# Hybrid decoder layer on eight cores: head-norm gains folded into the output gates, gated products left in PSUM, later side work, and a moved first weight load

## The chip, the cores and the metric

The kernel runs as one program on all eight NeuronCores of one Trainium2 chip. Each core takes one prompt of 2048 tokens and 16 samples of 4 tokens, so the cores do equal work on different data and do not talk to each other. The metric is the device time of the slowest core, in microseconds (us).

Some executions here were slower: the four cores of one die show a lower granted TensorE clock, 0.82 to 0.97 where the other die has 0.99 or 1.00. Each run below is marked fast or slow, and only fast runs are compared.

Names of engines in the profile: PE is TensorE's matrix multiplication and PEld its weight load, DVE is VectorE, ACT is ScalarE, POOL is GpSimd, SP is the engine that issues part of the transfers. PSUM (PS in the traces) is the memory that this program's matmuls write to, handed out by the program in eight banks; SBUF is the memory that holds its other tiles. An element of work in this kernel is usually a matmul with 512 columns, or an elementwise operation on a tile of 128 partitions by 512 float32 values (256 KB, 2 KB in each partition).

## The reference, cut to what matters

One layer, for a prompt group and a sample group with the same weights:

```python
h = x + 0.5 * swiglu(rmsnorm(x, norm_ffn1), w_ffn1_in, w_ffn1_out)
u = rmsnorm(h, norm_mix)
# u @ w_in gives q, k, v, r of two branches (gated linear attention, retention)
oa  = group_rmsnorm(oa, gn_gla, x.dtype) * jax.nn.silu(ra)      # gn_gla, gn_ret: the head norm weights
orr = group_rmsnorm(orr, gn_ret, x.dtype) * jax.nn.silu(gr)     # silu(ra), silu(gr): the output gates
mix = jax.nn.sigmoid(gate_a) * (oa @ w_out[:V_A]) + jax.nn.sigmoid(gate_r) * (orr @ w_out[V_A:])
h = h + mix
h = h + 0.5 * swiglu(rmsnorm(h, norm_ffn2), w_ffn2_in, w_ffn2_out)
h = h + (p @ w_ple_proj) * jax.nn.sigmoid(rmsnorm(h, norm_ple) @ w_ple_gate)    # input embedding
# after the layer: a final rmsnorm; the outputs are y and the new states
```

D_MODEL is 1024, the feed-forward width (FFN below) 2816, and there are four heads of value width 128 in each branch. A group norm of one block of 128 tokens therefore touches 4 heads x 128 value rows x 128 tokens.

## The kernel before

The program lists its operations with their estimated costs, and a list scheduler of its own then orders them on each engine, chooses buffers, and, for operations marked "flex", chooses between VectorE and GpSimd. So an edit in one place can move instructions elsewhere. The prompt is processed in two halves of two 512-token tiles; the sample group (64 tokens per core, "S" in tile names) is a third, small tile.

The start: activations are issued by the SP engine, the first two weight tiles, two pieces each, by GpSimd. A piece waits for the transfer named `first`, here the gains (GpSimd's first issue waits 3.0 us for it on core 6):

```python
first = dma("sp", gains[:], cpack[:], "c0", 34e3)
for q in range(4):
    xload(T[0].h, T[0], q, 4, ("x0", q))        # activations of the first tile, four pieces
xload(hS, T[4], 0, 1, "xS")                     # activations of the sample group
w0 = [piece(0, j, (first,)) for j in range(2)]  # first weight tile
w1 = [piece(1, j, (first,)) for j in range(2)]  # second weight tile
x1 = [xload(T[1].h, T[1], ..., (w1[0],)) for q in range(4)]   # second tile, after a weight piece
```

The end of an attention block: normalise, times the head norm weight, times the gate, one instruction for each head:

```python
tt(po, po, rs, ALU.mult, n)
for hl in range(4):
    gc = (G_GNA if br == 0 else G_GNR) + hl
    last = stt(t.q[br][:, hl, cs], po_.v(...), gains[:, gc:gc + 1], t.sr[br][:, hl, cs],
               ALU.mult, ALU.mult, bn)
```

The merge into the residual `h`. The gated product goes from PSUM into an SBUF buffer (`m1`, from a pool of 2 KB buffers called P2), and the add is "flex". The embedding stage has the same lines with `pp` for `pm`:

```python
S.limits = dict(..., gate=4, pm=3, ...)         # PSUM banks that a class of work may hold
(pg_, sg_), (pm_, m1_) = bundle("gate", PSUM, P2), bundle("pm", PSUM, P2)
... # pg: gate matmuls, sg: its tanh
... # pm: output projection matmuls
stt(m1, sg, 1.0, pm, ALU.add, ALU.mult, n)
tt(t.h[:, dm, :], t.h[:, dm, :], m1, ALU.add, n, eng="flex")
```

The second FFN of the first half is interleaved with `side`, a generator that emits what is left of the mixing, the states and the sample group's recurrence. One step of it is taken in every FFN step `k`. At the FFN's end the squares for the third tile's first normalisation are listed (`early[2] = full_norm(T[2])`), with nothing that keeps them from being scheduled earlier:

```python
for k, (g, t) in enumerate(seq):
    ...                                         # FFN matmuls of one group of columns
    if side is not None:
        next(side, None)
```

Of the kernel before, what the change touches and what calls it, by code (L numbers as in the profile page):

```python
# [30 lines left out]
TW = 2.5  # L31
BL = 150
# [632 lines left out]
def build_program():  # L665
# [100 lines left out]
    S.limits = dict(ffn=4, fo=3, fill=1, xp=2, qk=3, v=3, rg=2, gate=4, pm=3, po=2, sc=1, pu=1, ms=3, acc=3, accb=3, sq=3, mf=1, sqb=2, qt=1, up=1,  # L766
                    dec=6, rot=2, alow=1, st=4, tr=1, samp=3, sb=2, vb=1, pb=2)

    def bundle(cls, *pools):
        vts = [VT(p, cls) for p in pools]  # L770
        Bundle(vts, cls)
        return vts if len(vts) > 1 else vts[0]
# [13 lines left out]
    def act(out, in_, func, n, scale=1.0, bias=0.0):  # L786
        rd = [in_] + [x for x in (scale, bias) if not isinstance(x, float)]
        return S.op("act", lambda e: e.activation(out=res(out), in_=res(in_), func=func, bias=bias, scale=scale),  # L788
             rd, [out], dur=n * 0.000833 + (0.066 if inpsum(in_) else 0.095) + (0.0 if isinstance(scale, float) else 0.07), lat=0.2,
             tset=ACT_SET.get(func))  # L790
# [121 lines left out]
    first = dma("sp", gains[:], cpack[:], "c0", 34e3)  # L912
    for q in range(4):
        xload(T[0].h, T[0], q, 4, ("x0", q))
# [29 lines left out]
    class Norm:  # L944
        def __init__(self, t, direct=7, src=None):
            self.t, self.direct = t, direct
            self.src = t.h if src is None else src
            if direct:
                self.acc = bundle("acc", P2)

        def add(self, kc):
            t, n = self.t, self.t.n
            hk = self.src[:, kc, :]
            if kc < self.direct:

                a = self.acc.v(lambda x, n=n: x[:, 0:n])
                if kc == 0:
                    act(a, hk, AF.Square, n)
                    return
                q = bundle("sq", P2).v(lambda x, n=n: x[:, 0:n])  # L960
                act(q, hk, AF.Square, n)
                out = a
                if kc == self.direct - 1:
                    self.accb = bundle("accb", P1)
                    out = self.accb.v(lambda x, n=n: x[:, 0:n])
                tt(out, a, q, ALU.add, n, eng="flex")
                return
# [25 lines left out]
    def full_norm(t, direct=7, src=None):  # L993
        nm = Norm(t, direct, src)
        for kc in range(8 if direct < 7 else 7):
            nm.add(kc)
        return nm
# [3 lines left out]
    def ffn(tiles, next_gcol, lastk=LASTK, parts=None, then=None, side=None, plan=None, lead=None):  # L1001
# [5 lines left out]
        for k, (g, t) in enumerate(seq):  # L1007
# [14 lines left out]
            if side is not None:  # L1022
                next(side, None)
# [24 lines left out]
        if next_gcol == G_PLE and tiles[0].i == 0:  # L1048
            early[2] = full_norm(T[2])
# [15 lines left out]
    def mixing(hi, tiles, gtiles):  # L1065
# [111 lines left out]
        def rgate(t, r, br):  # L1177
            n = t.n
            for hl in range(4):
# [3 lines left out]
                act(t.sr[br][:, hl, :], p, AF.Silu, n)  # L1183

        def finish_o(t, br, b, po_, sqb_):
# [16 lines left out]
            for hl in range(4):  # L1202
                gc = (G_GNA if br == 0 else G_GNR) + hl
                last = stt(t.q[br][:, hl, cs], po_.v(lambda x, hl=hl, bn=bn: x[:, hl * bn:(hl + 1) * bn]),
                           gains[:, gc:gc + 1], t.sr[br][:, hl, cs], ALU.mult, ALU.mult, bn)
# [114 lines left out]
        def gate(t, br, dm, rg, ro):  # L1320
            n = t.n
            (pg_, sg_), (pm_, m1_) = bundle("gate", PSUM, P2), bundle("pm", PSUM, P2)
            pg, pm, sg, m1 = (x.v(lambda a, n=n: a[:, 0:n]) for x in (pg_, pm_, sg_, m1_))
# [7 lines left out]
            tt(t.h[:, dm, :], t.h[:, dm, :], m1, ALU.add, n, eng="flex")  # L1331
# [46 lines left out]
    def ple(hi):  # L1378
# [13 lines left out]
        def tile(t):  # L1392
# [6 lines left out]
            for dm in range(8):  # L1399
                (pg_, sg_), (pp_, m1_) = bundle("gate", PSUM, P2), bundle("pm", PSUM, P2)  # L1400
                pg, pp, sg, m1 = (x.v(lambda a, n=n: a[:, 0:n]) for x in (pg_, pp_, sg_, m1_))
# [11 lines left out]
                tt(t.h[:, dm, :], t.h[:, dm, :], m1, ALU.add, n, eng="flex")  # L1413
# [122 lines left out]
```

## Time and profile before

Three runs: 1512.15, 1514.57 and 1516.16 us, median 1514.57. The profiled run took 1515.37 us; its cores spanned 1506.6 to 1513.8 us.

| what | value | where read |
|---|---|---|
| TensorE busy | 97% of the span | page, part 1 |
| chain that ended last | 92% TensorE | page, part 4 |
| first FFN matmul starts | 24.8 to 27.7 us | timeline of each core |
| idle before the second FFN | 3.6 us, then a clock of 0.51 for 2.9 us | timeline, windows |
| VectorE, 512-column adds into `h` | 0.68 to 1.79 us | each such instruction, core 1 |

The page of the slowest core, number 6: its first line, the busy line of part 1 (engine, busy us, share, number of instructions), and the chain of work that ended last.

```profile
span 1513.8 us, 25283 instructions; the slowest of 8 cores (1506.6 to 1513.8 us)
PE 1465.8 (97%) x8720; PEld 709.7 (47%) x8875; DVE 682.4 (45%) x1330; ACT 565.6 (37%) x1053; POOL 197.4 (13%) x245
PE 92%; DVE 2%; issue 2%; ACT 2%; DMA 1%; SPq 0%; POOL 0%; DVEq 0%; ACTq 0%; POOLq 0%
```

TensorE bounds the kernel. No other engine matters by its busy time. Each can matter where TensorE waits for it, and a TensorE stall can cost twice, as the next lines show for this one: 3.61 us idle, and then matmuls at a lower clock. They are TensorE's timeline on core 6 (start, length of the merged group, operation, tiles; in brackets the idle time before it and what ended it).

```profile
487.79 3.19 PE L780 MATMUL PS<-u_47,ring_51 128*128 128x512 bf16 x14
494.58 0.57 PE L780 MATMUL PS<-T_2_100,ones 128*128 128x512 bf16 x1 [3.61 <-DVE T_2_100 L808]
...
495.37 4.73 PE L780 MATMUL PS<-u_47,ring_51 128*128 128x512 bf16 x15
```

Fourteen matmuls take 3.19 us before the stall of 3.61 us, and fifteen take 4.73 us after it: the granted clock is 1.00 from 485 us up to the stall, 0.51 from 494.6 to 497.5 us and 0.89 from there to 500 us. What it waited for stands in VectorE's timeline, same core:

```profile
489.51 1.12 DVE L808 TENSOR_TENSOR h_44<-h_44,T_0_104 128x512 f32<-128x512 f32 x1
...
491.34 1.43 DVE L808 TENSOR_TENSOR h_44<-h_44,T_7_111 128x512 f32<-128x512 f32 x1
492.69 1.75 DVE L808 TENSOR_TENSOR T_2_100<-T_11_115,T_0_104 128x512 bf16<-128x512 f32 x1
```

The same operation takes 0.69 us elsewhere. The window around it, with the columns' header (busy us and number of instructions of each engine, then the clock granted to TensorE and the share of DMA time):

```profile
core 6: us, PE busy (x) PEld busy (x) DVE busy (x) ACT busy (x) POOL busy (x), PEclk, DMA share, GB/s
475.00:500.00 25.00, 21.34 (x93) 9.02 (x93) 21.21 (x28) 17.29 (x27) 8.60 (x8) 0.93 0.44 73
```

A later wait on the same core, for work on the sample group (the prediction's third point):

```profile
547.88 0.30 PE L780 MATMUL PS<-T_8_112,kt_95 64*64 64x256 bf16 x2 [2.31 <-DVE T_8_112 L821]
```

```profile
27.50 1.89 PE L780 MATMUL PS<-u_47,ring_50 128*128 128x512 bf16 x8
```

### The profile page before, as it was taken

The numbers are of one execution on the slowest core, as the hardware profiler recorded it, in microseconds if no ns is written. First come the engines' busy times: TensorE is split into PE (matmuls) and PEld (weight loads), VectorE is DVE, ScalarE is ACT, GpSimd is POOL, SyncE is SP. The second block draws the span as 40 slices with busy tenths as digits, with TensorE's granted clock in tenths as the row PEclk, the third lists the DMA queues.
The fourth block names the chain that finished last, engine by engine and source line by source line (L and its number), as shares of the span: only waits on it lengthen the run. The fifth ranks groups of instructions, "written<-read, shape, count | busy, mean of one in ns | idle before, by whom it ended". The sixth has DMA issues, their size and how long they took to land.

```text
span 1513.8 us, 25283 instructions; the slowest of 8 cores (1506.6 to 1513.8 us)
## 1 busy us (share of the span) xinstructions
PE 1465.8 (97%) x8720; PEld 709.7 (47%) x8875; DVE 682.4 (45%) x1330; ACT 565.6 (37%) x1053; POOL 197.4 (13%) x245
## 2 busy tenths in 40 slices
PE   7999999999999999999999999999999999999996
PEld 2644444454444444444444444444444445444554
DVE  2322222649767633222683111253886752222367
ACT  3511111546765424311481111134675542121246
POOL 1000001002213100000230000000232310000032
PEclk8999999999999999999999999999999999999998
DMA  9833335441343486344677433544235326424104
GB/s 199 135 74 58 58 74 103 77 84 43 57 113 69 99 161 133 76 72 80 139 168 167 84 58 72 94 84 78 53 66 107 69 57 112 76 41 78 25 1 126
DMA packets 46860, 133.31 MB, mean 88 GB/s; under 512 B 5136, under 2 KB 27536, under 8 KB 37264
## 3 DMA queue, kind: packets, MB, share of 16 engines
q0 software_dynamic: 17616, 101.03, 38.1%
q1 hardware_dynamic: 29120, 30.65, 6.5%
q8 instruction: 74, 1.21, 0.3%
q14 instruction: 50, 0.41, 0.1%
HBM read 219.59 MB, written 13.11 MB: 154 GB/s over the span
## 4 chain that ended last, share of the span: by engine, by line
PE 92%; DVE 2%; issue 2%; ACT 2%; DMA 1%; SPq 0%; POOL 0%; DVEq 0%; ACTq 0%; POOLq 0%
PE PS L780 92%; DMA hS<-xP 1%; DVE u_47 L815 1%; ACT L788 1%; ACT PS L788 0%; PE PS L784 0%; SPq L838 0%; DVE T_2_100 L808 0%; DVE h_45 L815 0%; ACT T_0_104 L788 0%; DVE qR_90 L821 0%; DVE h_43 L815 0%; DVE T_0_104 L808 0%; DVE h_44 L808 0%; ACT T_9_113 L788 0%
## 5 line engine op out<-in xcount | busy, mean ns | idle before, releaser
L788 ACT ACT_TABLE_LOAD x90 | 115.5, 1283 | 27.5 <-PE PS L780 23.7
L780 PE MATMUL PS<-u_48,ring_54 128*128 128x512 bf16 x434 | 101.3, 384 | 0.7
L780 PE MATMUL PS<-u_47,ring_54 128*128 128x512 bf16 x436 | 100.3, 379 | 0.6
L780 PE MATMUL PS<-u_47,ring_52 128*128 128x512 bf16 x401 | 94.8, 379 | 0.8
L780 PE MATMUL PS<-u_48,ring_52 128*128 128x512 bf16 x406 | 94.1, 379 | 0.6
L780 PE MATMUL PS<-u_47,ring_50 128*128 128x512 bf16 x373 | 88.5, 379 | 0.7 <-issue 0.3
L780 PE MATMUL PS<-u_47,ring_51 128*128 128x512 bf16 x374 | 87.9, 383 | 0.6 <-issue 0.2
L780 PE MATMUL PS<-u_48,ring_50 128*128 128x512 bf16 (+1 forms) x407 | 86.4, 362 | 0.5
L780 PE MATMUL PS<-u_48,ring_51 128*128 128x512 bf16 (+1 forms) x410 | 85.6, 362 | 0.3
L780 PE MATMUL PS<-u_47,ring_53 128*128 128x512 bf16 x343 | 79.4, 379 | 0.5 <-issue 0.2
L780 PE MATMUL PS<-u_48,ring_53 128*128 128x512 bf16 x342 | 78.7, 379 | 0.7 <-ACT T_3_107 L788 0.2
L780 PEld LDWEIGHTS PS<-u_48,ring_54 128*128 128x128 bf16 x448 | 43.6, 99 | 52.5 <-issue 2.5
L780 PEld LDWEIGHTS PS<-u_47,ring_54 128*128 128x128 bf16 x448 | 42.7, 98 | 49.3 <-issue 1.1
L780 PEld LDWEIGHTS PS<-u_48,ring_52 128*128 128x128 bf16 x416 | 40.2, 98 | 47.8 <-issue 1.3
L780 PEld LDWEIGHTS PS<-u_48,ring_51 128*128 128x128 bf16 x416 | 40.5, 98 | 42.2 <-issue 0.4
L780 PEld LDWEIGHTS PS<-u_47,ring_52 128*128 128x128 bf16 x416 | 39.1, 98 | 44.8 <-issue 2.3
L780 PEld LDWEIGHTS PS<-u_48,ring_50 128*128 128x128 bf16 x416 | 40.3, 98 | 41.7 <-issue 0.2
L815 DVE SCALAR_TENSOR_TENSOR h_43<-PS,h_43 128x512 f32<-128x512 f32 (+2 forms) x37 | 22.7, 618 | 82.4 <-PE PS L780 77.4
L780 PEld LDWEIGHTS PS<-u_47,ring_51 128*128 128x128 bf16 x384 | 37.4, 99 | 45.1 <-issue 2.7
L780 PEld LDWEIGHTS PS<-u_47,ring_50 128*128 128x128 bf16 x384 | 36.9, 98 | 41.3 <-issue 0.4
L780 PEld LDWEIGHTS PS<-u_48,ring_53 128*128 128x128 bf16 x352 | 34.1, 98 | 40.6 <-issue 0.4
L780 PEld LDWEIGHTS PS<-u_47,ring_53 128*128 128x128 bf16 x352 | 33.5, 98 | 39.6 <-issue 1.9
(918 smaller groups left out, 2427.1 us busy)
## 6 DMA issues: line engine op xcount, KB each, us to landing
ring_52<-wflat POOLq DMA_DIRECT2D x14, 1024.0 KB, 9.8
ring_53<-wflat POOLq DMA_DIRECT2D x14, 1024.0 KB, 9.4
ring_54<-wflat POOLq DMA_DIRECT2D x14, 1024.0 KB, 9.3
ring_50<-wflat POOLq DMA_DIRECT2D x14, 1024.0 KB, 9.2
ring_51<-wflat POOLq DMA_DIRECT2D x12, 1024.0 KB, 9.1
ring_51<-wflat POOLq DMA_DIRECT2D x7, 704.0 KB, 6.0
ring_52<-wflat POOLq DMA_DIRECT2D x7, 704.0 KB, 6.1
ring_53<-wflat POOLq DMA_DIRECT2D x6, 704.0 KB, 6.4
```

The source lines that it names most:

```text
L780: return S.op("pe", lambda e: e.matmul(res(out), lhsT=res(lhsT), rhs=res(rhs), start=start, stop=stop, **kw), [lhsT, rhs], [out], dur=max( ...
L788: return S.op("act", lambda e: e.activation(out=res(out), in_=res(in_), func=func, bias=bias, scale=scale), rd, [out], dur=n * 0.000833 + ...
L815: return S.op("dve", lambda e: e.scalar_tensor_tensor(out=res(out), in0=res(in0), scalar=res(scalar), in1=res(in1), op0=op0, op1=op1), rd, ...
```

## The change

The intent, as its few words put it: head norm weights put into the output gates, gated products kept in PSUM, side work of the second FFN beginning later, the first weight load moved. In this document the four parts are called **gain**, **PSUM**, **side** and **first**. The diff, cut to its core (the embedding stage gets the same three edits as the merge; plumbing of the `after` argument is left out):

```diff
-    first = dma("sp", gains[:], cpack[:], "c0", 34e3)
-    for q in range(4):
-        xload(T[0].h, T[0], q, 4, ("x0", q))
+    dma("sp", gains[:], cpack[:], "c0", 34e3)
+    first = [xload(T[0].h, T[0], q, 4, ("x0", q)) for q in range(4)][0]
 ...
                 act(t.sr[br][:, hl, :], p, AF.Silu, n)
+                gc = (G_GNA if br == 0 else G_GNR) + hl
+                act(t.sr[br][:, hl, :], t.sr[br][:, hl, :], AF.Copy, n, scale=gains[:, gc:gc + 1])
 ...
-            for hl in range(4):
-                gc = (G_GNA if br == 0 else G_GNR) + hl
-                last = stt(t.q[br][:, hl, cs], po_.v(...), gains[:, gc:gc + 1], t.sr[br][:, hl, cs], ALU.mult, ALU.mult, bn)
+            last = tt(t.q[br][:, :, cs], po_.v(...), t.sr[br][:, :, cs], ALU.mult, n)
 ...
-    S.limits = dict(..., pm=3, ...)
+    S.limits = dict(..., pm=2, ...)
 ...
-            (pg_, sg_), (pm_, m1_) = bundle("gate", PSUM, P2), bundle("pm", PSUM, P2)
+            (pg_, sg_), pm_ = bundle("gate", PSUM, P2), bundle("pm", PSUM)
+            m1 = pm
 ...
-            tt(t.h[:, dm, :], t.h[:, dm, :], m1, ALU.add, n, eng="flex")
+            tt(t.h[:, dm, :], t.h[:, dm, :], m1, ALU.add, n)
 ...
+SKIP = 4
+EA = 1
-            if side is not None:
+            if k == SKIP:
+                mark["on"] = (S.ops[-1],)
+            if side is not None and k >= SKIP:
                 next(side, None)
 ...
-            early[2] = full_norm(T[2])
+            early[2] = full_norm(T[2], after=mark["on"] if EA else ())
```

More of the change, by code (lines that the diff above doesn't have):

```diff
@@ L765, in build_program @@
     S = Sched(bases)
-    S.limits = dict(ffn=4, fo=3, fill=1, xp=2, qk=3, v=3, rg=2, gate=4, pm=3, po=2, sc=1, pu=1, ms=3, acc=3, accb=3, sq=3, mf=1, sqb=2, qt=1, up=1,
+    S.limits = dict(ffn=4, fo=3, fill=1, xp=2, qk=3, v=3, rg=2, gate=4, pm=2, po=2, sc=1, pu=1, ms=3, acc=3, accb=3, sq=3, mf=1, sqb=2, qt=1, up=1,
                     dec=6, rot=2, alow=1, st=4, tr=1, samp=3, sb=2, vb=1, pb=2)
@@ L784, in transp, with act @@
         S.op("pe", lambda e: e.transpose(res(out), res(in_), res(idn)), [in_, idn], [out], dur=0.056, lat=0.265)
-    def act(out, in_, func, n, scale=1.0, bias=0.0):
+    def act(out, in_, func, n, scale=1.0, bias=0.0, after=()):
         rd = [in_] + [x for x in (scale, bias) if not isinstance(x, float)]
@@ L789, in act @@
              rd, [out], dur=n * 0.000833 + (0.066 if inpsum(in_) else 0.095) + (0.0 if isinstance(scale, float) else 0.07), lat=0.2,
-             tset=ACT_SET.get(func))
+             tset=ACT_SET.get(func), after=after)
     def acopy(out, in_, n, after=()):
@@ L944, in build_program, with __init__ @@
     class Norm:
-        def __init__(self, t, direct=7, src=None):
-            self.t, self.direct = t, direct
+        def __init__(self, t, direct=7, src=None, after=()):
+            self.t, self.direct, self.after = t, direct, after
             self.src = t.h if src is None else src
@@ L957, in add @@
                 if kc == 0:
-                    act(a, hk, AF.Square, n)
+                    act(a, hk, AF.Square, n, after=self.after)
                     return
                 q = bundle("sq", P2).v(lambda x, n=n: x[:, 0:n])
-                act(q, hk, AF.Square, n)
+                act(q, hk, AF.Square, n, after=self.after)
                 out = a
@@ L991, in to_u, with full_norm @@
             S.bias = 0
-    def full_norm(t, direct=7, src=None):
-        nm = Norm(t, direct, src)
+    def full_norm(t, direct=7, src=None, after=()):
+        nm = Norm(t, direct, src, after)
         for kc in range(8 if direct < 7 else 7):
@@ L1201, in finish_o @@
             cs = slice(b * 128, b * 128 + bn)
-            for hl in range(4):
-                gc = (G_GNA if br == 0 else G_GNR) + hl
-                last = stt(t.q[br][:, hl, cs], po_.v(lambda x, hl=hl, bn=bn: x[:, hl * bn:(hl + 1) * bn]),
-                           gains[:, gc:gc + 1], t.sr[br][:, hl, cs], ALU.mult, ALU.mult, bn)
+            last = tt(t.q[br][:, :, cs], po_.v(lambda x, n=n: x[:, 0:n].rearrange("p (h c) -> p h c", h=4)),
+                      t.sr[br][:, :, cs], ALU.mult, n)
             t.fin = (last,)
@@ L1321, in gate @@
             n = t.n
-            (pg_, sg_), (pm_, m1_) = bundle("gate", PSUM, P2), bundle("pm", PSUM, P2)
-            pg, pm, sg, m1 = (x.v(lambda a, n=n: a[:, 0:n]) for x in (pg_, pm_, sg_, m1_))
+            (pg_, sg_), pm_ = bundle("gate", PSUM, P2), bundle("pm", PSUM)
+            pg, pm, sg = (x.v(lambda a, n=n: a[:, 0:n]) for x in (pg_, pm_, sg_))
+            m1 = pm
             for kc in range(8):
@@ L1399, in tile @@
             for dm in range(8):
-                (pg_, sg_), (pp_, m1_) = bundle("gate", PSUM, P2), bundle("pm", PSUM, P2)
-                pg, pp, sg, m1 = (x.v(lambda a, n=n: a[:, 0:n]) for x in (pg_, pp_, sg_, m1_))
+                (pg_, sg_), pp_ = bundle("gate", PSUM, P2), bundle("pm", PSUM)
+                pg, pp, sg = (x.v(lambda a, n=n: a[:, 0:n]) for x in (pg_, pp_, sg_))
+                m1 = pp
                 wg = w[0 if dm < 4 else 2][:, :].rearrange("p (f k c) -> p f k c", k=8, c=128)
@@ L1412, in tile @@
                 stt(m1, sg, 1.0, pp, ALU.add, ALU.mult, n)
-                tt(t.h[:, dm, :], t.h[:, dm, :], m1, ALU.add, n, eng="flex")
+                tt(t.h[:, dm, :], t.h[:, dm, :], m1, ALU.add, n)
                 nm.add(dm)
```

## The prediction

> **What bounds the kernel now.** TensorE. The page shows PE 97% busy of 1513.8 us, VectorE 45%, ScalarE 37%; the chain of waits is 92% matmul. No large matmul is removed, so only PE's idle and slow-clock time can be won. On the profiled core (6), from the waits of PE, the timeline and the windows:
>
> - Start: the first FFN matmul begins at 27.7 us (24.8 on core 3, the fastest). It waited for the first normalisation, held up on ScalarE by the sample activations, which landed at 21 us, 16.4 us after issue, beside 4 MB (in the source) of weights. Those weights land 10 us before use.
> - Mixing to second FFN, 490.9 to 494.6 us: 3.6 us idle for one VectorE add (T_2_100). Sixteen matmuls then take about 0.43 us instead of 0.216: some 3 us at half clock. [...] the window's clock of 0.93 agrees. Before this stall residual adds ran on GpSimd (1.26 us), VectorE adds stretched from 0.69 to 1.1-1.8 us, and ScalarE squared the next tile (h_45).
> - 545.6 to 547.9: 2.3 us for sample states that landed 17 us after issue, with DMA 95% busy, and about 1.8 us of half clock. Most cores lack this.
> - Several waits of 0.5 to 1.8 us in attention, the embedding stage and the end, about 10 us.
>
> All mid-kernel losses together are about 25 us.
>
> **The change, costed.**
> - Head gain into the gate: 4 VectorE instructions of 0.28 us per block (1.12) become one of about 0.69; 32 blocks save some 14 us of VectorE. ScalarE gets 32 scalings of about 0.62 us (20 us). On the critical path: about 0 (+-2).
> - Gated product in PSUM, residual add always on VectorE: the add then has one SBUF input. [...] They should return to 0.69 us. But the two banks are held until the add is done, where three used to be: a risk of waits when an 8-instruction normalisation (5.4 us) sits in front.
> - Side work four steps later, h_45's squares deferred: empties the engines just where the 3.6 us stall is.
> - First weights wait for the first activation piece (about 7 us instead of 3.3): activations land about 3 us sooner; the weights have slack.
>
> **Sum.** Start -3; stall at 490 and its cold clock -5 (of 6.5); DMA stall -1; PSUM banks, ScalarE and tail +0.5. About -8.5 us, 0.6%.
>
> **Prediction:** 1506 us, 8 in 10 between 1498 and 1513. Faster by over 2% (below 1485): 0.01, since it exceeds all idle time reachable. Within 2%: 0.98. Slower by over 2%: 0.01.
>
> **Right if** the first FFN matmul starts near 24.5 us on all cores; PE is at 24 of 25 us or more and clock about 1.0 around the second FFN's start; additions into h take 0.69 us and none is on GpSimd; ScalarE busy rises about 20 us.
>
> **Wrong if** PE newly waits for PSUM additions in the gate or embedding stages (two banks); if the scaling delays attention on ScalarE; if PE waits for the first weights; or if the deferred squares only move the stall to where the third tile is normalised. The program orders its instructions by its own list scheduler, so unrelated places may shift by 1 or 2 us.

Two passages are cut, where marked. -3 -5 -1 +0.5 makes the -8.5 us. "The window's clock of 0.93 agrees" is the window of 25 us printed above, with 0.51 just after the stall. "They should return to 0.69 us" (the adds of 1.1 to 1.8 us) stands as the estimate. The trace of before supports it: on core 6 the 512-column VectorE operations of this kind (TENSOR_TENSOR) with one input in PSUM took 0.69 us in the mean, 19 of them beside GpSimd work (at most 0.70) and 247 with GpSimd idle.

## More of the kernel before

A norm adds up its squares with further "flex" additions of two SBUF operands. GpSimd therefore has elementwise work even where it adds nothing into `h`.

The start of core 1: the waits of TensorE up to 30 us, the longest two lines; the first FFN matmul in the timeline; and the two DMA queues from 12 to 17 us, where q0 carries the weights and q1 the activations (packets, MB, share of the time of the 16 DMA engines).

```profile
PE PS L780 <- ACT T_0_98 L788: 4.6, 2, 3.0
PE PS L780 <- DVE Sbf L835: 2.7, 1, 2.7
```

```profile
q0 software_dynamic: 163, 0.60, 71.0%
q1 hardware_dynamic: 163, 0.52, 29.9%
```

T_0_98 holds the square of a piece of activations: the wait is really one for the transfer of that piece.

## The result, and the profile after

Four runs: 1493.50, 1493.67, 1493.92 and 1493.95 us, median 1493.8, against 1515.37 us, the median of four runs of before (the three above and one more of 1517.17). All are fast, with a granted clock of 0.995 to 0.997 on every core. The ratio is 0.986, with a 95% interval of 0.9842 to 0.9877. Here and below a ratio is the mean time of one kernel's fast runs over that of the other's of the same rounds, so not quite the ratio of the medians that are quoted. Executions in which one die ran at a lower clock are left out of the means. The change won 21.6 us by the medians, 1.4%. "Within 2%" was right, but the time lies 4 us below the low end of the predicted range.

The page of the slowest core after, number 1:

```profile
span 1491.9 us, 25299 instructions; the slowest of 8 cores (1489.9 to 1491.9 us)
PE 1468.5 (98%) x8875; PEld 708.5 (47%) x8875; DVE 666.2 (45%) x1281; ACT 578.2 (39%) x1084; POOL 136.2 (9%) x192
PE 93%; DVE 2%; ACT 1%; issue 1%; DMA 1%; POOL 0%; DVEq 0%; SPq 0%; ACTq 0%; POOLq 0%
```

TensorE's timeline before the second FFN, and its window:

```profile
481.12 3.19 PE L782 MATMUL PS<-u_47,ring_51 128*128 128x512 bf16 x14
484.60 0.38 PE L782 MATMUL PS<-T_5_103,ones 128*128 128x512 bf16 x1 [0.29 <-DVE T_5_103 L810]
```

```profile
475.00:500.00 25.00, 24.71 (x116) 11.08 (x114) 17.13 (x28) 10.52 (x16) 2.38 (x3) 1.00 0.49 86
```

The 3.61 us are 0.29 us now, and the clock is whole. The start of core 1: the longest two waits, the first FFN matmul, and the queues from 7 to 12 us.

```profile
PE PS L782 <- DVE Sbf L837: 2.7, 1, 2.7
PE PS L782 <- ACT T_0_98 L790: 1.5, 1, 1.5
```

```profile
19.22 1.89 PE L782 MATMUL PS<-u_47,ring_50 128*128 128x512 bf16 x8
```

```profile
q1 hardware_dynamic: 459, 1.51, 94.1%
q0 software_dynamic: 4, 0.02, 1.8%
```

The first FFN matmul starts 8.3 us sooner on this core (over the cores: 16.6 to 19.2 us, where it was 24.8 to 27.7). The activations had nearly the whole of the DMA to themselves: 94.1% of the time of the 16 engines, and 1.51 MB in these 5 us.

The elementwise work, by group of instructions (busy us, mean ns of one, idle before): first a finishing product of before on core 6, then the new one, the new scalings on ScalarE and an addition into `h`, on core 1 of after.

```profile
L815 DVE SCALAR_TENSOR_TENSOR qR_79<-PS,gains,sr 128x128 bf16<-128x128 f32 x32 | 9.0, 344 | 0.5
```

```profile
L810 DVE TENSOR_TENSOR qR_79<-PS,sr 128x512 bf16<-128x512 f32 x8 | 5.5, 689 | 0.6
L790 ACT ACTIVATE sr<-sr,gains 128x512 f32<-128x512 f32 x16 | 11.3, 722 | 1.1
L810 DVE TENSOR_TENSOR h_43<-h_43,PS 128x512 f32<-128x512 f32 x40 | 26.8, 683 | 1.8
```

### Where the time came from

For each core whose trace has a record of every matmul, I took the start of each matmul and subtracted the ideal time of the program's matmuls before it: 216 ns for 512 columns, as they follow each other in the trace at full clock, in proportion for fewer columns, but not below 29 ns (the 64-column matmuls follow each other after 29 ns in the trace of core 1); the filler matmuls of the start are left out. What remains is TensorE time lost up to that point, idle or at a lower clock. The columns cut the program at fixed amounts of matmul work, so at the same stages in every kernel: the start up to 25 us of matmul work; the first FFN and the first half's mixing up to 450; the second FFN of the first half up to 625; its end and the embedding up to 750; the second half's first FFN and attention up to 1125; the rest. Only differences between rows are read. (A figure can be negative, since the ideal time is only an estimate for small matmuls.) The mean is over the six of the eight cores with complete records; before and after these are the same six, all but cores 0 and 6 (the experiments' six are partly others).

```
us of TensorE lost    start  to 450  450-625  625-750  750-1125   rest   mean span
before                 27.8     8.4      2.0      1.7       7.4   15.8      1509.0
after                  19.8     7.9     -3.1      0.8       5.9   14.1      1491.2
difference             -8.0    -0.5     -5.1     -0.9      -1.5   -1.7       -17.8
```

The differences add up to the 17.7 us that the mean core won (17.8 unrounded). The slowest core of the profiled run won 21.9 (1513.8 to 1491.9), since it lay 4.8 us above this mean before and 0.7 us after.

### The profile page after: what moved, and what is told of

The parts are those of the page before. It is cut to its first block, busy times and chain, and to the rows that moved or that the text cites. A ratio compares the mean times of both kernels' runs of the same rounds, so it can differ in the third digit from the quotient of the medians.

```text
span 1491.9 us, 25299 instructions; the slowest of 8 cores (1489.9 to 1491.9 us)
## 1 busy us (share of the span) xinstructions
PE 1468.5 (98%) x8875; PEld 708.5 (47%) x8875; DVE 666.2 (45%) x1281; ACT 578.2 (39%) x1084; POOL 136.2 (9%) x192
## 4 chain that ended last, share of the span: by engine, by line
PE 93%; DVE 2%; ACT 1%; issue 1%; DMA 1%; POOL 0%; DVEq 0%; SPq 0%; ACTq 0%; POOLq 0%
PE PS L782 93%; DVE u_47 L817 1%; ACT L790 1%; DMA h_43<-xP 0%; ACT PS L790 0%; DMA rtab_116<-rtab 0%; PE PS L786 0%; POOL T_2_100 L810 0%; DVE T_5_109 L810 0%; DVE h_43 L817 0%; DVE qR_90 L823 0%; DVE T_0_104 L810 0%; DVE T_10_114 L810 0%; DVE PS L817 0%; DVE T_2_106 L810 0%
## 5 line engine op out<-in xcount | busy, mean ns | idle before, releaser
L790 ACT ACT_TABLE_LOAD x81 | 103.9, 1283 | 23.3 <-PE PS L782 20.5
L782 PE MATMUL PS<-u_47,ring_54 128*128 128x512 bf16 x448 | 103.1, 379 | 0.0
L782 PE MATMUL PS<-u_48,ring_54 128*128 128x512 bf16 x448 | 100.8, 379 | 0.0
L782 PE MATMUL PS<-u_47,ring_52 128*128 128x512 bf16 x416 | 97.0, 379 | 0.0
L782 PE MATMUL PS<-u_48,ring_52 128*128 128x512 bf16 x416 | 94.6, 379 | 0.1
L782 PE MATMUL PS<-u_47,ring_50 128*128 128x512 bf16 x384 | 89.8, 379 | 0.0
L782 PE MATMUL PS<-u_47,ring_51 128*128 128x512 bf16 x384 | 87.8, 379 | 0.0
L782 PE MATMUL PS<-u_47,ring_53 128*128 128x512 bf16 x352 | 81.7, 379 | 0.1
L782 PE MATMUL PS<-u_48,ring_53 128*128 128x512 bf16 x352 | 79.4, 379 | 0.0
L782 PEld LDWEIGHTS PS<-u_48,ring_54 128*128 128x128 bf16 x448 | 43.6, 98 | 51.4 <-issue 0.4
L782 PEld LDWEIGHTS PS<-u_47,ring_54 128*128 128x128 bf16 x448 | 42.3, 98 | 47.4 <-issue 0.7
L782 PEld LDWEIGHTS PS<-u_48,ring_52 128*128 128x128 bf16 x416 | 40.5, 98 | 48.4 <-issue 1.2
L782 PEld LDWEIGHTS PS<-u_48,ring_51 128*128 128x128 bf16 x416 | 40.5, 98 | 42.2 <-issue 0.4
L782 PEld LDWEIGHTS PS<-u_47,ring_52 128*128 128x128 bf16 x416 | 39.2, 98 | 44.5 <-issue 2.0
L782 PEld LDWEIGHTS PS<-u_48,ring_50 128*128 128x128 bf16 x416 | 40.0, 98 | 41.9 <-issue 0.7
L782 PEld LDWEIGHTS PS<-u_47,ring_51 128*128 128x128 bf16 x384 | 37.1, 98 | 43.8 <-issue 0.8
L782 PEld LDWEIGHTS PS<-u_47,ring_50 128*128 128x128 bf16 x384 | 36.6, 98 | 41.2 <-issue 1.4
L782 PEld LDWEIGHTS PS<-u_48,ring_53 128*128 128x128 bf16 x352 | 34.1, 98 | 40.5 <-issue 0.4
L790 ACT ACTIVATE PS<-PS 128x512 f32<-128x512 f32 (+4 forms) x90 | 44.9, 509 | 20.1 <-PE PS L782 16.7
```

What stands on the lines that cost most here:

```text
L782: return S.op("pe", lambda e: e.matmul(res(out), lhsT=res(lhsT), rhs=res(rhs), start=start, stop=stop, **kw), [lhsT, rhs], [out], dur=max( ...
L790: return S.op("act", lambda e: e.activation(out=res(out), in_=res(in_), func=func, bias=bias, scale=scale), rd, [out], dur=n * 0.000833 + ...
```

## The experiments

Two kinds: one part of the change put into the kernel before (labels with d), and one part taken out of the changed kernel (labels with u). Every result was correct. Every kernel was timed against runs of the kernel before on the same chip; medians below are of the fast runs (15 of the 77 executions of the experiments were slow and are left out). The chips differ a little: the median of before was 1513.0 to 1513.9 us on four occasions and 1517.2 us on one chip, of which more below. Letters in the quoted expectations name theories; where it helps they are explained after the quotes.

The table of losses for the experiments on undisturbed chips, in the same columns (two cores each of d_first and d_pm2 had one stretch of 4 us at a clock of 0.81, which costs under 1 us):

```
us of TensorE lost    start  to 450  450-625  625-750  750-1125   rest   mean span
d_first                19.9     8.7      3.1      1.8       7.6   15.8      1502.7
d_gain                 27.3     8.4      1.7      1.9       5.2   16.2      1506.5
d_psum                 27.4     8.2     -3.0      1.2       7.5   14.3      1501.5
d_side                 27.4     8.2     -2.5      1.8       7.4   16.3      1504.5
d_pm2                  27.7     8.0      1.1      2.0       6.2   18.2      1509.1
u_first                27.4     7.9     -3.1      0.8       5.9   14.1      1498.8
u_gain                 20.0     8.2     -3.1      0.8       7.1   14.4      1493.2
u_psum                 19.6     8.0     -2.2      1.8       5.5   15.5      1493.9
u_side                 19.4     7.9     -3.2      1.4       5.9   14.2      1491.3
u_hold                 19.2     7.9     -3.1      0.8       5.9   13.9      1490.5
u_tosb_pm2             19.8     7.7     -3.0      2.6       5.2   18.4      1496.4
u_pm3                  19.7     7.5     -3.2      4.6       6.2   16.9      1497.6
u_tosb2                19.6     7.9     -2.4      6.0       5.7   18.1      1500.9
u_vec                  20.1     9.4     -2.0      6.3      12.4   22.1      1514.0
```

### The moved first weight load: d_first, u_first

d_first is the kernel before with the first hunk of the diff alone; u_first is the changed kernel with that hunk undone.

```diff
-    first = dma("sp", gains[:], cpack[:], "c0", 34e3)
+    first = [xload(T[0].h, T[0], q, 4, ("x0", q)) for q in range(4)][0]
```

> The kernel before with one edit: the first weight pieces wait for the first activation piece instead of the gains. The order of instructions on every engine is unchanged by it (compared before this run), so only the wait differs. Theory (the weight reads took the larger share of the DMA engines from the activations of the first normalisation, which were needed first; the weights had slack): the sample activations land near 13 us instead of 21, the weights at the same times as before (about 16, 19, 23, 26 us), the first FFN matmul starts near 18 to 19 us, and the whole is 8 to 9 us faster, about 1507 us; every stage after the start loses what it lost before. Rival (the two queues share evenly, as the prediction assumed; the rest of the early gain comes from the other edits' reordering): 3 us faster, about 1512, first matmul near 24.5.

> The changed kernel with only this edit undone (again the same order on every engine). Theory: 8 to 9 us slower than the changed kernel, about 1502, and the cores spread again by some 3 us, because their start depends on when the activations land. Rival: about 1497.

Measured: d_first 1506.06 us (1505.79 to 1512.21, three fast runs), ratio 0.9964 with an interval of 0.9932 to 0.9995; u_first 1502.3 us (four fast runs), ratio 0.9919 (0.9904 to 0.9934). The order of the instructions of d_first is that of before on every engine, so only the wait differs. The start column shows it alone: 27.8 to 19.9 us when it is added, 19.8 to 27.4 us when it is taken away. So this part is worth some 8 us at the start, alone and in company; of the mean span it wins 6.3 us alone and costs 7.6 us when taken away. Most of the rest of the 8 us in d_first is lost again in the second FFN (3.1 us against 2.0), where the expectation had no change: the single cores of the profiled run have 1.5 to 5.2 us there, and core 7 waits 2.0 us for work on the sample group, as core 6 does before. One of the three fast runs came out 6 us longer than the others, by one core (core 3, 1510.7 us). That run has no trace, so its cause is not shown.

### Why so much at the start: d_half, u_late

In d_half, the kernel before lets the second weight tile alone wait for the first activation piece; the first weight tile goes as early as before. In u_late, the changed kernel lets all weights wait for the fourth activation piece instead of the first.

```diff
 d_half, from before:
-    w1 = [piece(1, j, (first,)) for j in range(2)]
+    w1 = [piece(1, j, (xfirst,)) for j in range(2)]     # xfirst: the first activation piece
 u_late, from after:
-    first = [xload(T[0].h, T[0], q, 4, ("x0", q)) for q in range(4)][0]
+    first = [xload(T[0].h, T[0], q, 4, ("x0", q)) for q in range(4)][3]
```

> The kernel before, with only the second weight (two pieces) made to wait for the first activation piece; the first weight still starts at once. Same order on every engine. Theory Q (weight pieces are served one after the other, and whichever is being served takes most of the DMA engines; the first weight alone is busy until about 19 us): the activations land as late as before, sample activations at 19 to 21 us, first FFN matmul 25 to 28 us, total 1513 to 1516. Rival V (the activations are slowed in proportion to all the weight bytes in flight): half the gain, sample activations near 17 us, first matmul near 23, total about 1510.

> The changed kernel with the weights held for the last (fourth) activation piece, about 12 us, instead of the first, about 7 us. The scheduler moves some filler matmuls at the start with it. Theory: the activations hardly land sooner (12 to 13 us, as in the changed kernel), the weights land 3 to 4 us later, their slack is used up, and the second tile's activations, which wait for the second weight, land later too; first FFN matmul near 20 to 21 us, total 1495 to 1498. Rival (the weights' time still doesn't matter): 1493 to 1495.

These ran, with d_noflex and u_tosb, on a chip where TensorE's clock fell to 0.81 in stretches even in fast runs: a 512-column matmul then follows the last after 263 ns and not 216. On core 2 of u_late the granted clock is 0.81 from 740 to 750 us, 1.00 from 755 to 765 us and 0.81 again from 775 to 780 us, with TensorE busy for 39.9 of the 40 us. That cost up to 8 us on single cores, so times are compared within this chip only, where before took 1517.2 us. The start column is early enough to be free of it.

Measured: d_half 1519.6 us, ratio 1.0012 (0.9989 to 1.0035), start 27.5 us: no gain. u_late 1507.0 us, ratio 0.9929 (0.9907 to 0.9952), start 27.9 us: the whole 8 us are gone, which the expectation had not seen (it had the first matmul right, at 20 to 21 us, and a loss of 2 to 4 us in all). Times from issue to landing on core 1 explain all four (each entry is the moment of issue > the moment of landing, in us, worked out from the trace's transfer records):

```
            4th piece, tile 0   samples       weight pieces (2 of tile 0, 2 of tile 1)              tile 1, last
before      2.9>17.0            3.5>20.8      3.8>15.4   4.5>19.0   5.0>22.7   5.5>25.9             25.2>34.3
d_half      2.9>17.6            4.7>21.3      3.7>15.4   4.4>18.8   8.1>22.5   8.7>25.7             25.0>34.2
after       2.9>12.4            4.5>13.1      7.9>16.3   8.6>19.5   9.2>22.9   9.7>25.7             25.4>33.5
u_late      2.9>12.2            4.2>12.8     12.8>20.1  13.5>24.0  14.0>27.1  14.5>30.8             28.7>38.2
```

Three things are seen here. Before, the first weight piece overlaps the activations; from 12 to 17 us the two queues moved 163 packets each (core 1; 177 and 164 on core 0, 159 and 156 on core 6), but the weight packets took 71% of the time, so the activations crawled: 0.52 MB in these 5 us, where after moves 1.51 MB from 7 to 12 us. With 5 us of 16 engines, a weight packet took 0.35 us (71% of 80 us, over 163) and an activation packet 0.15 us; for the packets of 4096 bytes alone it is 0.39 and 0.18 us. Second, the weight pieces land one after another, 3.2 to 3.7 us apart in before. d_half issues the second tile's pieces 3.1 us later, and the activations land no sooner (17.6 and 21.3 us, against 17.0 and 20.8), so it is the first tile's pieces that matter. Third, in after the weights land within 0.9 us of where they landed before, although issued 4.1 us later; the first packet of the first piece came 5.3 us after its issue in before, 4.0 us in after and 2.6 us in u_late (core 1; why these waits differ, no run here shows). The later start used up their slack: in u_late the first piece lands 3.8 us later still, and the second tile's activations, which wait behind a weight piece, 4.7 us later. TensorE's timeline of u_late on core 1, and its window:

```profile
22.52 11.82 PE L782 MATMUL PS<-u,ring 128*128 128x512 bf16 x54
...
45.37 10.84 PE L782 MATMUL PS<-u,ring 128*128 128x256 bf16 x76 [3.54 <-DVE u L817]
```

```profile
45.00:50.00 5.00, 4.63 (x22) 2.54 (x23) 4.70 (x14) 4.65 (x8) 0.00 (x0) 0.50 1.04 174
```

The first FFN matmul waits until 22.5 us (19.2 in after; over the cores 18.5 to 22.5, mean 20.0, where after has 18.2), and at 45.4 us the normalised second tile is 3.5 us late, and TensorE is at half clock from 43.4 to 50.2 us (0.50 in the window). So only some 2 of the 8 us are the first tile's; most are the second tile's wait and the half clock with it. The change's choice, the first piece, is right between the two that were tried.

### Gains in the gates: d_gain, u_gain

The second and third hunks of the diff, alone in before, and undone in after:

```diff
+                act(t.sr[br][:, hl, :], t.sr[br][:, hl, :], AF.Copy, n, scale=gains[:, gc:gc + 1])
-            for hl in range(4):
-                last = stt(..., gains[:, gc:gc + 1], t.sr[br][:, hl, cs], ALU.mult, ALU.mult, bn)
+            last = tt(t.q[br][:, :, cs], po_.v(...), t.sr[br][:, :, cs], ALU.mult, n)
```

> The kernel before with the head norm weights folded into the gates alone (32 large ScalarE scalings more, one VectorE product in place of four per block). Theory A (neither engine bounds the attention stages for long): 1513 to 1517, within 2 us of before, changes only between the two attention stages. Rival B (the shorter VectorE chain in attention frees TensorE): 3 us faster or more, with the waits of TensorE in the attention stage of the second half gone. Rival C (ScalarE, 24 of 25 us busy there, becomes the limit): 2 us slower or more.

> The changed kernel with the fold undone. Theory A: within 2 us of the changed kernel, 1492 to 1496. Rival B: 1497 or more. Rival C: 1492 or less.

Measured: u_gain 1496.8 us (three fast runs), ratio 0.9882 (0.9865 to 0.9898). d_gain had only one fast run, 1509.68 us; its other three were slow (up to 1742 us, one die at a clock of 0.84), so it has no ratio and is read from its profile, which is of the fast run. Both say the same: about 2 us in the mean span (1509.0 to 1506.5; 1493.2 against 1491.2), most of it in the second half's attention (7.4 to 5.2; 7.1 against 5.9), where the prediction had 0. So theory A, no change, is missed by both; d_gain's one run lies 4 us under the median of before on its chip, as rival B had it, and u_gain at 1496.8 just under B's line of 1497. Rival C, ScalarE as the new limit, falls. The windows over that stage on core 1, before and then d_gain:

```profile
1010.00:1185.00 175.00, 170.98 (x1079) 81.09 (x1078) 122.12 (x262) 101.03 (x187) 34.43 (x40) 1.00 0.42 76
```

```profile
1010.00:1185.00 175.00, 173.37 (x1119) 83.54 (x1118) 115.49 (x223) 114.60 (x210) 37.41 (x43) 1.00 0.42 75
```

VectorE has 6.6 us less to do, ScalarE 13.6 us more, and TensorE is busy 2.4 us more. The window ends after different work in the two, so the table is the better measure of the size; the direction is the same. In the first half's attention little or nothing was won (8.4 and 8.4 us; 8.2 against 7.9).

### The product in PSUM, and the side work: d_psum, u_psum, d_side, u_side

d_psum has the three edits of the PSUM part in both stages and nothing else; d_side has the SKIP and EA lines and nothing else. u_psum and u_side undo them.

```diff
 d_psum: pm=3 becomes pm=2; m1 = pm (and m1 = pp); eng="flex" taken from the two adds into h
 u_side: SKIP = 0 and EA = 0 in the changed kernel
```

> The kernel before with the gated products kept in PSUM and the residual add fixed on VectorE alone (two product banks instead of three). Theory P (the 3.6 us stall before the second FFN and the half-clock matmuls after it come from residual adds on GpSimd and from VectorE adds stretched by GpSimd): that stall is under 1 us, the embedding stage loses about 1 us less, total about 1508 to 1510. Rival S (they come from the third tile's squares and the sample work that crowd ScalarE and VectorE just then): the stall stays, total 1513 or more. Rival B (two banks are too few): new waits of TensorE on VectorE in the gates, total above 1516.

> The changed kernel with this part undone. Theory P: the stall of 3 us or more is back before the second FFN, about 1499. Rival S: stays below 1496.

> The kernel before with the later side work and the deferred squares alone. Theory P: the stall before the second FFN stays at 2 us or more, since the adds on GpSimd remain; total 1512 to 1515. Rival S: the stall goes, total about 1509 to 1510.

> The changed kernel with the side work begun at once and the squares not deferred. Theory P: below 1496. Rival S: 1498 or more, the stall of 3 us or more is back. If both d_psum and d_side remove the stall, either suffices; if neither does, both are needed.

| kernel | median us | ratio to before, 95% interval |
|---|---|---|
| d_psum | 1505.2 | 0.9945 (0.9930 to 0.9961) |
| u_psum | 1497.4 | 0.9893 (0.9875 to 0.9911) |
| d_side | 1509.1 | 0.9970 (0.9949 to 0.9992) |
| u_side | 1494.5 | 0.9874 (0.9859 to 0.9890) |

Either part alone removes the loss in the second FFN stage: 2.0 us becomes -3.0 with PSUM and -2.5 with side, and in company -3.1. Taking either away leaves it removed (-2.2 and -3.2). So theory P (the adds alone make the stall) is refuted by d_side and u_psum, rival S (the side work alone makes it) by d_psum and u_side, and rival B (two banks are too few) by d_psum. The windows on core 1 (before has 21.39 us busy and a clock of 0.93 there, and a stall of 3.61 us), of d_psum and then d_side, and the one wait of TensorE that d_side has left in its window:

```profile
475.00:500.00 25.00, 24.93 (x139) 11.39 (x138) 21.87 (x33) 19.29 (x30) 7.45 (x7) 1.00 0.55 106
```

```profile
475.00:500.00 25.00, 23.99 (x115) 10.66 (x113) 18.26 (x28) 14.75 (x21) 6.80 (x6) 1.00 0.50 85
491.64 0.59 PE L782 MATMUL PS<-T,ones 128*128 128x512 bf16 x2 [1.01 <-POOL T L810]
```

They are two cures for one stall, so their gains must not be added: alone they win 7.5 and 4.5 us of mean span, taken away they cost 2.7 and 0.2 us. The four parts taken away one by one cost 7.6, 2.0, 2.7 and 0.2 us, 12.5 of the 17.8; what is left is about the 5.1 us of this stage, which no single removal brings back.

What PSUM has and side has not is the embedding stage and the end: the two columns are 1.2 and 14.3 in d_psum, 1.8 and 16.3 in d_side, and 1.8 and 15.5 in u_psum against 0.8 and 14.1 in after. What side has and PSUM has not is evenness: d_side shows -2.5 us on each of its six cores, after -3.1 on each, while d_psum ranges from -3.4 to -2.0, u_side has one core at -2.0 and five at -3.4, and u_psum one at -0.7 and five at -2.5. Those are waits of 1.1 to 1.7 us on single cores, between 550 and 564 us. That they are for sample states, like the 2.3 us on core 6 that the prediction named, is likely but was not followed up. So side may do a little for the slowest of eight where it does nothing for the mean. With u_side at 1494.5 us and after at 1493.8, measured on other occasions, it is 0.7 us by the medians and 2 us by the ratios, whose intervals overlap: no gain of side in company is shown.

### Is it the adds, or that GpSimd has none of them: d_noflex, u_tosb

d_noflex is before with its adds into `h` fixed to VectorE, products still in SBUF. u_tosb is after with products in SBUF and three PSUM banks again, adds on VectorE.

```diff
 d_noflex: -tt(t.h[:, dm, :], ..., m1, ALU.add, n, eng="flex")   +tt(t.h[:, dm, :], ..., m1, ALU.add, n)
 u_tosb:   bundle("pm", PSUM, P2) with its m1, and pm=3, as in before; the add as in after
```

> The kernel before with the residual adds of the gates and the embedding fixed on VectorE, the products still in SBUF (three buffers and banks). Theory G (it is GpSimd's slow turn in the chain that made the 3.6 us stall): the stall goes as in d_psum, total within 2 us of d_psum, 1504 to 1508. Rival P1 (the SBUF product itself matters: two SBUF inputs are stretched while GpSimd works, and tiles are short): VectorE adds into h still take over 0.9 us on average, the stall stays at 2 us or more, total 1510 or more.

> The changed kernel with the product back in SBUF and the add still on VectorE. Theory G: within 1 us of the changed kernel (1493 to 1495). Rival P1: close to u_psum, 1497 to 1499, the losses of the embedding stage and of the tail back.

Measured on the disturbed chip: d_noflex 1522.1 us, ratio 1.0029 (1.0007 to 1.0052), so no better than before; u_tosb 1510.3 us, ratio 0.9949 (0.9926 to 0.9972). The stall before the second FFN is still there in d_noflex (no core of it has a stretch at 0.81 before 745 us):

```profile
493.78 1.01 PE L780 MATMUL PS<-T,ones 128*128 128x512 bf16 x2 [4.28 <-POOL T L808]
```

So taking the adds off GpSimd is not what wins, and theory G falls; u_tosb came out above what either theory had, and so did its repeat on another chip (u_tosb2, 1506.3 us, below). The durations say why. I split the adds into `h` of 512 columns on VectorE by whether a GpSimd tile operation ran at the same time for over 0.1 us:

```
adds into h on VectorE, 512 columns    GpSimd idle: count, mean ns    GpSimd at work: count, mean (max) ns
before      (product in SBUF)          26, 692                        24, 1259 (1787)
d_noflex    (product in SBUF)          64, 686                        24, 1349 (1804)
u_tosb_pm2  (product in SBUF)          63, 688                        25, 1327 (1908)
d_psum      (product in PSUM)          65, 684                        23,  684 (689)
after       (product in PSUM)          66, 684                        22,  683 (689)
```

With both inputs in SBUF an add takes nearly twice as long beside GpSimd work (1.26 to 1.35 us against 0.69). With one input in PSUM it takes 0.68 us, with GpSimd at work or idle; and GpSimd still does the additions of the norms. The ends of the slow adds show what they wait for: on core 1 of before, 23 adds overlap one GpSimd tile operation that ends first, and each of them ends 0.55 us after that operation (0.546 to 0.560), although they start 0.02 to 1.03 us into it. The same holds for 21 adds of u_tosb_pm2 (0.545 to 0.558). So in these two traces such an add waits for the end of the GpSimd operation, whenever it starts.

### Banks, buffers or adds: u_hold, u_vec, u_tosb2, u_pm3

u_tosb still mixed three things: the place of the product, the SBUF buffer it takes, and the number of banks. All four kernels start from after. u_tosb2 is u_tosb again, on a chip without the clock disturbance.

```diff
 u_hold:  +bundle("pm", PSUM, P2): the buffer is held as long as the product, and not used
 u_vec:   as u_tosb, and every other eng="flex" becomes eng="dve"
 u_pm3:   -pm=2  +pm=3
```

> The changed kernel with its product in PSUM, but each gate also holds an unused 2 KB SBUF buffer for as long as the product lives. Theory B (the product in SBUF cost time because it occupied the 12 SBUF buffers that squares, sigmoids and the sample states also need): the time rises to that of the kernel with the product in SBUF, about +10 us over the changed kernel, with 1 us stalls of TensorE in the embedding stage and at the end. Theory S (what cost time was the stretched addition, two SBUF inputs beside a busy GpSimd): within 2 us of the changed kernel, 1492 to 1496 us on an undisturbed chip, additions into h at most 0.69 us.

> The changed kernel with its product in SBUF, and all elementwise work on VectorE, none on GpSimd. Theory S: the additions into h take 0.69 us each although both inputs lie in SBUF, since GpSimd no longer runs beside them, and most of the loss of the product in SBUF goes, 1493 to 1498 us. Theory B: the buffers are as short as before, so 1500 to 1506 us with the same stalls in the embedding stage.

> The same kernel as u_tosb, for a chip whose granted clock is not disturbed: the comparison for the two others of this call. Expected about 1501 to 1505 us, with 3 us or more lost in the embedding stage of the second half and some 3 us at the end of attention.

> The changed kernel with three PSUM banks for gated products where it has two. The prediction named the two banks as a risk. If they cost something the time falls by 0.5 us or more against the changed kernel; if they cost nothing it is within 1 us, 1492 to 1495 us on an undisturbed chip.

| kernel | median us | ratio to before, 95% interval |
|---|---|---|
| u_hold | 1493.1 | 0.9869 (0.9853 to 0.9885) |
| u_vec | 1517.6 | 1.0027 (1.0012 to 1.0043) |
| u_tosb2 | 1506.3 | 0.9956 (0.9938 to 0.9974) |
| u_pm3 | 1500.8 | 0.9920 (0.9904 to 0.9935) |

The buffer is not it: u_hold is as fast as after, and theory B falls. It also runs the same instructions as after in the same order on VectorE, ScalarE and GpSimd, so it is nearly a second measurement of the change, on another chip: 0.9869, some 20 us. u_vec missed theory S's number as well: its adds take 0.685 us each, 88 of 88, and yet it loses, with all the work that was "flex" now on VectorE: 12.4 us in the second half's attention, where after loses 5.9, and 22.1 in the rest, where after loses 14.1. That run shows that getting rid of the contention was no gain here, bought with VectorE time. It neither supports nor refutes S. u_tosb2 is 1 us above its expected range. And u_pm3 was a surprise: with the product in PSUM, a third bank costs some 7 us (1500.8 us, against 1493.1 of u_hold on the same chip and 1493.8 of after). It loses in the embedding stage, 4.6 against 0.8 us, and at the end, 16.9 against 14.1. On core 1 the embedding stage has one new stall:

```profile
765.66 0.59 PE L782 MATMUL PS<-T,ones 128*128 128x512 bf16 x2 [2.12 <-POOL T L810]
```

and the windows around it, after first and then u_pm3:

```profile
750.00:775.00 25.00, 24.85 (x115) 10.72 (x113) 25.00 (x40) 18.40 (x29) 4.90 (x5) 1.00 0.96 212
```

```profile
750.00:775.00 25.00, 22.50 (x94) 9.54 (x94) 21.85 (x36) 20.18 (x28) 4.94 (x5) 0.93 0.98 211
```

2.1 us of waiting for one addition of a norm, placed on GpSimd, and the lower clock that follows (0.93 over the window). VectorE is full here (25.0 of 25 us in after), so the stage turns on the order in which the scheduler serves it.

### The place alone and the banks alone: u_tosb_pm2, d_pm2

```diff
 u_tosb_pm2, from after: bundle("pm", PSUM, P2) with its m1 in SBUF; two banks and the add on VectorE stay
 d_pm2, from before:     -pm=3  +pm=2
```

> The changed kernel with its product in SBUF, additions on VectorE and two PSUM banks: from the changed kernel it differs only in where the product lies. Theory S (what the product in PSUM wins is that additions no longer stretch beside GpSimd work): 24 or so of 88 additions stretch to 1.2 us or more, and the time is 5 us or more over the changed kernel, 1498 to 1506 us. Theory C (what counts is two banks instead of three): within 2 us of the changed kernel, 1492 to 1496 us, though the additions stretch.

> The kernel before with two PSUM banks for gated products instead of three, and nothing else. Theory C: the 3.6 us stall before the second FFN and the losses at the end go as with the whole PSUM part, 1503 to 1507 us. Theory S: the stall and the slow additions stay, 1510 to 1516 us, perhaps slower.

Measured on one chip: u_tosb_pm2 1499.6 us, ratio 0.9906 (0.9889 to 0.9924), where after and u_hold have 0.986 and 0.9869; d_pm2 1513.1 us, ratio 0.9997 (0.9982 to 1.0013). Two banks in the kernel before are worth nothing; its stall stays (3.27 us on core 1, now for an addition on GpSimd), and its end gets 2.4 us longer. The place of the product is worth 5 to 6 us at two banks (1499.6 against 1493.8 by the clock, 5.2 of mean span): 1.8 us in the embedding stage, 4.3 at the end, less 0.7 in attention. So theory C, that the bank count is what counts, falls as the whole explanation, and the time that S gave is right. That the stretched additions are what costs those 5 to 6 us is still not isolated. The program's scheduler reckons with such a wait itself (an operation with two SBUF inputs gets `lock` in its cost model), so with the product in SBUF it makes another schedule: the traces of u_tosb_pm2 and after differ in order on every engine, and nine operations have moved from VectorE to GpSimd (1281 to 1272, 192 to 201). What is shown is the worth of the place together with the schedule that it brings; u_pm3 shows that a schedule alone can cost 7 us. The groups of the additions, d_psum and then u_tosb_pm2:

```profile
L808 DVE TENSOR_TENSOR h<-h,PS 128x512 f32<-128x512 f32 x88 | 59.0, 684 | 4.3
```

```profile
L810 DVE TENSOR_TENSOR h<-h,T 128x512 f32<-128x512 f32 x88 | 74.9, 870 | 3.4
```

The same 88 additions cost VectorE 15.9 us more with the product in SBUF. Place and banks also work together: with the product in PSUM the third bank costs some 7 us, with the product in SBUF some 7 us too (1506.3 in u_tosb2 against 1499.6 in u_tosb_pm2, by ratios 0.9956 and 0.9906 on two chips; 4.5 us of mean span), in the kernel before nothing. Why the scheduler's order suffers from the third bank is not shown by these runs; they show where it loses and how much. No version that was tried beats the change by more than the spread of its runs: u_hold, at 1493.1 us on its chip, is equal to it.

## Why the prediction was wrong

- **The bound was right.** TensorE is 97% busy before and 98% after, and no more than idle and slow-clock time was won.
- **The start was right in mechanism and wrong in size: -3 us predicted, -8.0 measured.** The step that failed is "activations land about 3 us sooner". The prediction gives only the shift of the weights' issue (7 us instead of 3.3) beside its 3 us, so that shift seems to have been its bound of the gain. The trace of before had the better sum: from 12 to 17 us the weights' queue held 71% of the DMA time. With that taken away until it is needed, the sample activations land 7.7 us sooner (20.8 to 13.1 on core 1). "The weights have slack" was right, and u_late shows that what was used is about all of it. The check "near 24.5 us on all cores" was wrong: 16.6 to 19.2 us.
- **The stall at 490 us and the DMA stall were right: -5 and -1 predicted, -5.1 measured for the stage on the mean core.** The 3.61 us are 0.29 and the window's clock is 1.00, as said. The DMA stall of 2.31 us on core 6 is gone too: no wait from 500 to 600 us is longer than 0.2 us on that core of after. What the prediction had not seen is that two parts of the change each cure it alone.
- **"PSUM banks, ScalarE and tail +0.5" had the wrong sign.** The step that failed is that the change can only cost there. The stages it stood for gave -0.9 in the embedding, -1.5 in the second attention (the gain part's, by u_gain) and -1.7 in the rest, and -0.5 before. The feared cost of two banks did not come; a third bank costs 7 us (u_pm3). The additions were correctly expected at 0.69 us (0.68 measured, none on GpSimd), but their worth was counted only at the 490 us stall. u_tosb_pm2 shows that the product's place, with the schedule that it brings, is worth 5 to 6 us in the embedding stage and at the end.
- **The gain part: "on the critical path about 0 (+-2)" measured -2.** That is at the edge of the range given. The VectorE sum was also small: a block's four products take 4 x 0.343 = 1.37 us by the groups of before and not 1.12, so 32 blocks save (1.37 - 0.69) x 32 = 22 us, not 14. ScalarE's scaling takes 0.72 us and not 0.62; the 32 cost 23 us. ScalarE's busy time rose by 12.6 us only, not "about 20": it reloads its function tables 81 times instead of 90 in the two profiles, which takes 103.9 us instead of 115.5.
- **The slowest of eight was not priced.** The metric is the slowest core. Over 25 fast runs of before on the undisturbed chips for which the cores were listed, it lay 1.9 to 6.3 us above the mean of the eight, 2 to 4 in most; after the change it lay 0.9 to 1.5 above in four runs. That is some 1.5 to 2 us of the gain, and 4.1 in the profiled runs (4.8 less 0.7, against the mean of six cores). The side part and the start, both of which remove waits for transfers, are where the cores differed most; that they are the cause of the evenness is likely by the per-core figures, but not separately shown.

Sum: -8.5 predicted; on the mean core -8.0 -0.5 -5.1 -0.9 -1.5 -1.7 = -17.7 measured. Of the 9.2 us that were missed, 5.0 are the start and 5.1 the four small stages (-4.6 measured, +0.5 predicted), less 0.9 by which the stall's stage gave less than was predicted.

## What to carry to other kernels

At the start of a kernel, look up in the trace which queue holds the DMA while the first compute waits (here the weights', 71% of the time), and hold back what is not needed until the first piece has landed; hold it no longer than its own slack. When GpSimd and VectorE both do elementwise work, try leaving one operand of VectorE's additions in PSUM: here the additions beside GpSimd work took 0.68 us so, and 1.26 to 1.35 us with both operands in SBUF, without giving up GpSimd. Do not add up the gains of parts that cure the same stall, and test a "safe" resource limit in both directions.
